# Attention values in three reduced-precision products per block, with split operands and smaller pools

## The chip, the cores and the metric

The kernel runs on one core of a Trainium2 chip. The core has a matrix engine (PE; its weight loads are shown apart as PEld), a vector engine (DVE), a scalar engine (ACT), a general engine (POOL), and an engine that here only issues DMAs (SP; its queue is SPq). Each takes its instructions in the order in which the program gives them. The metric is the device time of one execution in microseconds; a kernel's time is the median of several runs.

## The reference, cut to what matters

One step of a hybrid layer (a state-space branch, a differential-attention branch, a convolutional feed-forward part) runs over a prompt of 1024 positions and 64 sampled positions that have 512 cached ones. All arithmetic is in float32. The change lies in the attention:

```python
def _diff_attn_block(q, k, v, q_pos, k_pos, lam):
    s = jnp.einsum('bqhd,bkhd->bhqk', q, k) * (ATT_HEAD_DIM ** -0.5)
    s = jnp.where(visible[None, None], s, -jnp.inf)
    p = jax.nn.softmax(s, axis=-1).reshape(b, ATT_HEADS, 2, nq, -1)
    a = p[:, :, 0] - lam * p[:, :, 1]
    return jnp.einsum('bhqk,bkhe->bqhe', a.astype(v.dtype), v)
```

There are 8 heads; a head's values are 128 wide, and queries are taken in blocks of 128.

## The kernel before, in words

Names first. `F32` is float32; `R32` is a reduced form of it in the same four bytes. A product in full precision (both operands F32) is one instruction in the program and two MATMUL records in the trace. Where the kernel wants nearly full precision from R32 operands it splits each into a high part (a cast to R32, made on ACT) and a low part (the float32 value less the high part, made on DVE), and adds three products in one PSUM bank: high by high, high by low, low by high (`product`, L153 to L158). The input projections are all of this kind: one tile of 128 outputs by 384 or 320 positions is 8 times three MATMULs.

**Attention** (L659 to L821) goes head by head, and in a head over nine units, in the order of `ATT_ORDER`: unit i < 8 is the i-th block of 128 queries with 128(i+1) keys, unit 8 is the 64 sampled queries with 576 keys. `head_tiles` (L661) fetches a head's queries, keys and values; the values were `v_t` (nine blocks of 128 rows, two buffers) and `cv_t` (four blocks of cached values, one buffer). `attend` (L682) makes the scores with R32 operands (L707, L708, the high and the low part of the keys against the same stationary `q_t`), takes row maxima on DVE (L712, L716) and exponentials on ACT (L721, into `p_t`, four buffers), joins the two softmaxes on DVE (L725), and then, a step later, transposes the result by blocks of 128 keys on PE (L736, full precision, into the PSUM tile `pt`, four blocks to a tile), copies each `pt` to `a_t` (L741 on ACT and L743 or L745 on DVE, by turns) and multiplies it by the values (L755): one product of 128 moving columns a block, in full precision, with the block of `a_t` as the stationary operand. A head has 1+2+...+8 = 36 such blocks and 5 of unit 8, so 8 heads have 328. ACT then copies the sum out (L756) and squares it (L757). `head_out` (L760) norms a head's output, transposes it (L777), splits it (L780, L781) and stores it.

**What lies between.** Attention alone does not fill PE. `fill` draws from `stream()`, a row of projection tiles (convolution inputs, z, gates), 1.9 tiles a unit. Each is emptied from one of two PSUM banks by ACT or ACT and DVE; `conv_tiles` (L608) goes on from there with `pre` (two buffers) and `cc` (three), four DVE operations, one more ACT operation and a store on SP.

**Order.** The program is written in Python order, but a scheduler with its own table of costs puts the instructions of each engine into one fixed order when the kernel is built. So PE meets attention and projections interleaved in that order, and waits where an operand is late. Buffers of a pool are reused in turn, and a wait for a buffer stands in the queue of the engine that writes it next; for a DMA this is SP's queue, in which the loads of projection weights (`w_f`, L142) and the stores of `cc` (L635) stand too.

Of the kernel before, what the change touches and what calls it, by code (L numbers as in the profile page):

```python
# [9 lines left out]
F32 = mybir.dt.float32  # L10
R32 = mybir.dt.float32r
AF = mybir.ActivationFunctionType
ALU = mybir.AluOpType
# [4 lines left out]
P = 128  # L18
D = 1024
KT = D // P  # L20
TP, TS = 1024, 64
T = TP + TS
# [3 lines left out]
LAMBDA_INIT = 0.8 - 0.6 * math.exp(0.0)  # L26
# [21 lines left out]
QSQ = 1  # L48
QUICK = 400
IDLE = (9, 8)  # L50
AT = 4
AHEAD_IN = 100
AHEAD = 100
ZR = 3
# [16 lines left out]
O_FS, O_SUB, O_LAM = 408, 452, 580  # L71
# [4 lines left out]
def hybrid_layer(ctx: ExitStack, tc: tile.TileContext, xT, xN, prm, cst, rope, wvd, win, wbs, wba, wout, wup, wdn,  # L76
                 ckT, cv, st0, yT, kT, v, ssm, conv, ffn):
    nc = tc.nc
    V, S, G, PE = nc.vector, nc.scalar, nc.gpsimd, nc.tensor
    act = S.activation  # L80
    load = nc.sync.dma_start
# [16 lines left out]
    par = cp.tile([P, N_PRM], F32, name="par")  # L98
# [193 lines left out]
    with tc.tile_pool(name="nx", bufs=1) as nx:  # L292
# [116 lines left out]
        w = [raw_weights(wvd[0], 4, 272), raw_weights(wvd[1], 4, 272)]  # L409
# [7 lines left out]
        a, b = halves  # L417
# [166 lines left out]
    cv_pool = tc.alloc_tile_pool(name="cv", bufs=1, side="right")  # L584
# [23 lines left out]
    def conv_tiles(tiles):  # L608
        for f in tiles:
            tail = None  # L610

            def evac(ps, c, w):
                nonlocal tail
                n = min(w, TP - c)
                pre = cv_pool.tile([P, 387], F32, name="pre", tag="pre", bufs=2)
                cc = cv_pool.tile([P, 384], F32, name="cc", tag="cc", bufs=3)
                if tail is None:
                    G.memset(pre[:, 0:3], 0.0)  # L618
                else:
# [10 lines left out]
                act(cc[:, :m], pre[:, :m], AF.Identity, bias=col(O_CB + f), scale=cw(0))  # L630
# [4 lines left out]
                load(out=x_sc[P * f : P * (f + 1), c : c + n], in_=cc[:, :n])  # L635
# [23 lines left out]
    with (tc.tile_pool(name="ak", bufs=1) as ak, tc.tile_pool(name="at", bufs=1) as at,  # L659
          tc.tile_pool(name="psc", bufs=1, space=PSUM) as psc, tc.tile_pool(name="psa", bufs=1, space=PSUM) as pa):  # L660
        def head_tiles(h):  # L661
            def fetch(name, n, b, parts):
                t = ak.tile([P, n], R32, name=name, tag=name, bufs=b)
                for lo, src in parts:
                    load(out=t[lo : lo + src.shape[0]].bitcast(F32), in_=src)
                return t

            by_head = lambda d: [d.rearrange("(x h) t -> h x t", h=16)[2 * h + c] for c in range(2)]
            q, k, ck = by_head(q_st), by_head(k_st), by_head(c_st)
            q_t = [fetch("q_t", T, 3, [(0, q[0])]), fetch("q_t", T, 3, [(0, q[1][64:128]), (64, q[1][0:64])])]  # L670
            kh_t = [fetch("kh_t", T, 3, [(0, k[c][0:64]), (64, k[c][0:64])]) for c in range(2)]
            kl_t = [fetch("kl_t", T, 3, [(0, k[c][64:128]), (64, k[c][64:128])]) for c in range(2)]
            v_t = ak.tile([P, 9, P], F32, name="v_t", tag="v_t", bufs=2)
            load(out=v_t[:, :8], in_=v[0:TP, P * h : P * (h + 1)].rearrange("(a p) e -> p a e", p=P))
            load(out=v_t[:TS, 8], in_=v[TP:T, P * h : P * (h + 1)])
            ch_t = [fetch("ch_t", PAST, 2, [(0, ck[c][0:64]), (64, ck[c][0:64])]) for c in range(2)]
            cl_t = [fetch("cl_t", PAST, 2, [(0, ck[c][64:128]), (64, ck[c][64:128])]) for c in range(2)]
            cv_t = ak.tile([P, 4, P], F32, name="cv_t", tag="cv_t", bufs=1)
            load(out=cv_t, in_=cv[:, P * h : P * (h + 1)].rearrange("(a p) e -> p a e", p=P))
            return q_t, kh_t, kl_t, ch_t, cl_t, v_t, cv_t  # L680

        def attend(h, i, tiles, o_t, ssq, s0):  # L682
            q_t, kh_t, kl_t, ch_t, cl_t, v_t, cv_t = tiles
# [6 lines left out]
            for c in range(2):  # L690
# [7 lines left out]
                for a in range(0, nk, 512):  # L698
                    b = min(512, nk - a)
# [28 lines left out]
            nb = -(-nk // P)  # L728
            for b0 in range(0, nb, 4):
                pt = pa.tile([P, 512], F32, name="pt", tag="pt", bufs=2)  # L730
                a4 = at.tile([P, 512], F32, name="a_t", tag="a_t", bufs=AT)
                a_t.append(a4)
                full = 0
                for b in range(b0, min(nb, b0 + 4)):
                    kw = min(P, nk - b * P)
                    PE.transpose(pt[:kw, (b - b0) * P : (b - b0) * P + n], pr[1][:n, b * P : b * P + kw], ident[:n, :n])  # L736
                    full += kw == P
                m3 = lambda x, k: x.rearrange("p (a b) -> p a b", b=P)[:, :k, :n]
                if full:
                    if (i + b0 // 4) % 2:  # L740
                        S.copy(m3(a4, full), m3(pt, full))  # L741
                    else:
                        V.tensor_copy(m3(a4, full), m3(pt, full))  # L743
                else:
                    V.tensor_copy(a4[:TS, :n], pt[:TS, :n])  # L745
            po = pa.tile([P, 512], F32, name="po", tag="pt", bufs=2)
            for b in range(nb):
                kw = min(P, nk - b * P)
                if i < 8:
                    rhs = v_t[:, b]  # L750
                elif b < 4:
                    rhs = cv_t[:, b]
                else:
                    rhs = v_t[:TS, 8]
                PE.matmul(po[:n, :P], a_t[b // 4][:kw, b % 4 * P : b % 4 * P + n], rhs, start=b == 0, stop=b == nb - 1)  # L755
# [4 lines left out]
        def head_out(h, o_t, ssq, s0):  # L760
            ms, rs, t0, t1 = (at.tile([P, 9], F32, name=n, tag=n, bufs=2) for n in ("ms", "ors", "on0", "on1"))
            V.tensor_tensor(out=ms, in0=s0, in1=s0, op=ALU.mult)
            V.tensor_scalar(ms, ms, EPS * 128, None, ALU.mult)
            V.tensor_tensor(out=ms, in0=ms, in1=ssq, op=ALU.add)
            act(t0, ms, AF.Ln, scale=1.0 / 128)
            act(t0, t0, AF.Exp, scale=-0.5)
            V.tensor_scalar(ms, ms, -0.5 / 128, None, ALU.mult)
            V.tensor_tensor(out=ms, in0=ms, in1=t0, op=ALU.mult)
            V.tensor_tensor(out=t1, in0=ms, in1=t0, op=ALU.mult)
            V.scalar_tensor_tensor(rs, t1, 1.5, t0, ALU.add, ALU.mult)  # L770
            for b0 in range(0, 9, 4):
# [7 lines left out]
                hi, lo = (at.tile([P, 512], R32, name=n, tag="a_t", bufs=AT)[:, :w] for n in ("oh", "ol"))  # L779
                S.copy(hi, pt[:, :w])  # L780
                V.tensor_tensor(out=lo, in0=pt[:, :w], in1=hi, op=ALU.subtract)  # L781
# [5 lines left out]
        lt = at.tile([P, 512], F32, name="lt", tag="a_t", bufs=AT)[:, :64]  # L787
# [807 lines left out]
```

## Time and profile before

| | us |
|---|---|
| median of 3 runs | 2453.19 |
| lowest, highest run | 2453.03, 2457.49 |
| the profiled execution's own time | 2448.89 |
| its span, first to last instruction | 2447.1 |
| attention: first scores to last value product | 400.2 to 1080.0 |
| PE idle over the whole span (2447.1 less 2423.5 busy) | 23.6 |

The page divides the span by engine: share of time busy, and number of instructions. The views used below are: the busy time of every engine in given stretches; groups of instructions by line and shape (count, busy time, mean duration of one); who waited for whom; and the timeline (start, duration, engine, line, shape). A MATMUL's duration in the timeline covers its way through the array, so neighbours overlap; what one costs PE is the step from its start to the next one's start.

### The profile page before, as it was taken

The page shows a single profiled execution, that of the slowest core. Times are in us where ns is not written, and L with a number is a line of the kernel's source. Part 1 is how long each engine was busy: PE and PEld are TensorE (multiplying, and loading weights), DVE is VectorE, ACT ScalarE, POOL GpSimd, SP SyncE. Part 2 cuts the span into 40 slices and gives each one's busy share as a digit, 9 for nine tenths or more (in the row PEclk, how much of TensorE's full clock was granted, in tenths as well). Part 3 has the DMA queues.
Part 4 walks back from the last instruction along what each step waited for, and adds up shares of the span by engine and source line. Part 5 has one row for each costly group of instructions (what it writes and reads, how often), then busy time and mean ns, then how long its engine had stood idle before and what let it go on. Part 6 is the DMA issues. An engine that isn't in the chain of part 4 may idle for free. (4 is left out here: it accounts for less than half of the span.)

```text
span 2447.1 us, 44586 instructions
## 1 busy us (share of the span) xinstructions
PE 2423.5 (99%) x16956; PEld 2350.1 (96%) x16956; DVE 1602.0 (65%) x2755; ACT 1139.8 (47%) x2497; POOL 664.8 (27%) x696
## 2 busy tenths in 40 slices
PE   9999999999999999999999999999999999999998
PEld 8999999999999999999899989999999999999998
DVE  7426254865777667646767785656777777787766
ACT  6334243644565555437664653224543334353532
POOL 0000000100011001004333333103367666755434
PEclk9999999999999999999999999999999999999999
DMA  4218158554453453345679765656234343467874
GB/s 172 84 57 288 64 207 265 142 158 126 131 162 110 130 169 104 98 157 186 217 255 323 223 199 186 193 176 189 63 125 140 117 153 116 147 202 207 218 181 159
DMA packets 269319, 403.55 MB, mean 165 GB/s; under 512 B 33296, under 2 KB 202000, under 8 KB 268976
## 3 DMA queue, kind: packets, MB, share of 16 engines
q1 hardware_dynamic: 258432, 385.06, 49.6%
q0 software_dynamic: 4608, 8.91, 2.4%
q10 hardware_dynamic: 6064, 6.72, 0.8%
q8 instruction: 133, 2.18, 0.4%
q14 instruction: 82, 0.67, 0.1%
HBM read 267.04 MB, written 133.56 MB: 164 GB/s over the span
## 5 line engine op out<-in xcount | busy, mean ns | idle before, releaser
L156 PE MATMUL mm<-xn_hi,w_hi 128*128 128x384 f32 (+1 forms) x1416 | 469.9, 332 | 0.9 <-DVE zr L603 0.9
L158 PE MATMUL mm<-xn_hi,w_lo 128*128 128x384 f32 (+1 forms) x1416 | 468.6, 331 | 0.5 <-DVE w_lo L150 0.5
L157 PE MATMUL mm<-xn_lo,w_hi 128*128 128x384 f32 (+1 forms) x1416 | 467.7, 330 | 0.0
L156 PEld LDWEIGHTS mm<-xn_hi,w_hi 128*128 128x128 f32 x1416 | 266.7, 188 | 4.8 <-issue 1.6
L158 PEld LDWEIGHTS mm<-xn_hi,w_lo 128*128 128x128 f32 x1416 | 266.5, 188 | 3.4 <-issue 1.5
L157 PEld LDWEIGHTS mm<-xn_lo,w_hi 128*128 128x128 f32 x1416 | 266.7, 188 | 2.3 <-issue 1.1
L150 DVE TENSOR_TENSOR w_lo<-w_f,w_hi 128x1024 fp32r<-128x1024 f32 x116 | 147.1, 1270 | 117.9 <-ACT w_hi L149 117.5
L1254 PE MATMUL mx<-n,wh 128*128 128x272 f32 x1076 | 206.0, 289 | 0.7 <-ACT u L1398 0.4
L1254 PE MATMUL mx<-m,w_hi 128*128 128x272 f32 x1010 | 192.9, 289 | 4.2 <-DVE down L1412 4.2
L149 ACT CAST w_hi<-w_f 128x1024 fp32r<-128x1024 f32 x116 | 121.4, 1048 | 145.2 <-PE mm L157 87.5
L1254 PEld LDWEIGHTS mx<-n,wh 128*128 128x128 f32 x1076 | 169.2, 189 | 1.1 <-ACT u L1398 0.6
L1254 PEld LDWEIGHTS mx<-m,w_hi 128*128 128x128 f32 x1010 | 159.3, 189 | 4.6 <-issue 2.8
L1254 PE MATMUL mx<-n,wl 128*128 128x272 f32 x538 | 155.6, 289 | 0.0
L156 PE MATMUL mm<-b_hi,w_hi 128*128 128x384 f32 (+1 forms) x448 | 145.8, 327 | 0.6 <-DVE b_g L224 0.6
L1254 PE MATMUL mx<-m,w_lo 128*128 128x272 f32 x505 | 145.9, 289 | 0.0
L158 PE MATMUL mm<-b_hi,w_lo 128*128 128x384 f32 (+1 forms) x448 | 144.8, 324 | 0.6 <-DVE w_lo L150 0.6
L157 PE MATMUL mm<-b_lo,w_hi 128*128 128x384 f32 (+1 forms) x448 | 145.1, 325 | 0.0
L721 ACT ACTIVATE p_t<-sc,mx 128x1024 f32<-128x1024 f32 (+5 forms) x144 | 106.2, 739 | 76.4 <-DVE mx L712 37.5
L632 DVE SCALAR_TENSOR_TENSOR cc<-pre,par,cc 128x384 f32<-128x384 f32 (+1 forms) x216 | 126.6, 586 | 20.1 <-ACT cc L630 14.9
L620 POOL COPY pre<-pre 128x3 f32<-128x3 f32 x48 | 13.6, 282 | 454.5 <-ACT pre L621 343.6
L1039 ACT CAST w_hi<-ws 128x512 fp32r<-128x512 f32 (+1 forms) x62 | 37.6, 607 | 150.0 <-PE mx L1254 99.2
L618 POOL MEMSET pre<- 128x3 f32 x24 | 2.4, 101 | 383.9 <-PE mx L158 308.5
(418 smaller groups left out, 6735.7 us busy)
## 6 DMA issues: line engine op xcount, KB each, us to landing
w_f<-in_win_dram SPq DMA_DIRECT2D x76, 512.0 KB, 4.1
w_f<-in_wup_dram SPq DMA_DIRECT2D x44, 512.0 KB, 3.8
hr<-q_sc SPq DMA_DIRECT2D x70, 272.0 KB, 4.8
bc<-a_sc SPq DMA_DIRECT2D x32, 512.0 KB, 5.9
q_sc<-hb SPq DMA_DIRECT2D x44, 272.0 KB, 2.3
gb<-q_sc SPq DMA_DIRECT2D x44, 272.0 KB, 3.8
x_sc<-cc SPq DMA_DIRECT2D x48, 192.0 KB, 2.5
q_sc<-gb SPq DMA_DIRECT2D x33, 272.0 KB, 2.3
```

The costliest lines, as they stand in the source:

```text
L149: S.copy(hi, w)
L150: lowered = V.tensor_tensor(out=lo, in0=w, in1=hi, op=ALU.subtract)
L156: PE.matmul(ps, a_hi, b_hi, start=i == 0, stop=False)
L157: PE.matmul(ps, a_hi, b_lo, start=False, stop=False)
L158: PE.matmul(ps, a_lo, b_hi, start=False, stop=i == n - 1)
L618: G.memset(pre[:, 0:3], 0.0)
L620: G.tensor_copy(pre[:, 0:3], tail)
L632: V.scalar_tensor_tensor(cc[:, :m], pre[:, i : i + m], cw(i), cc[:, :m], ALU.mult, ALU.add)
L721: act(p_t[:n, :nk], sc[c][:n, :nk], AF.Exp, bias=mx[:n, c : c + 1], accum_out=dst)
L1039: S.copy(hi, src)
L1254: PE.matmul(ps, w[x][:, c], b[y][:, k], start=start and k == t == 0, stop=k == nk - 1 and t == 2, skip_group_check=not start)
```

## The change

The full-precision value product becomes three R32 products. For that, the transposed probabilities are split into `a_hi` (cast on ACT) and `a_lo` (difference on DVE), for every `pt`, where one copy on one of the two engines stood; and a head's values are split into `v_hi` and `v_lo`, once a head, 13 blocks of 128 rows each (prompt, cache, sample), in one buffer each. The float32 values that are split are loaded into two of the four `p_t` buffers. Where four `a_t` buffers stood, there are two `a_hi` and two `a_lo`. `cc` has two buffers in place of three, and the scaled norm weights `wsub` are made in place in `par`.

```diff
-AT = 4
+AT = 2
...
-                cc = cv_pool.tile([P, 384], F32, name="cc", tag="cc", bufs=3)
+                cc = cv_pool.tile([P, 384], F32, name="cc", tag="cc", bufs=2)
...
-            v_t = ak.tile([P, 9, P], F32, name="v_t", tag="v_t", bufs=2)
-            load(out=v_t[:, :8], in_=v[0:TP, P * h : P * (h + 1)].rearrange("(a p) e -> p a e", p=P))
-            load(out=v_t[:TS, 8], in_=v[TP:T, P * h : P * (h + 1)])
+            v_f = [at.tile([P, 8, P], F32, name="v_f", tag="p_t", bufs=4) for _ in range(2)]
+            load(out=v_f[0], in_=v[0:TP, P * h : P * (h + 1)].rearrange("(a p) e -> p a e", p=P))
+            load(out=v_f[1][:TS, 4], in_=v[TP:T, P * h : P * (h + 1)])
...
-            cv_t = ak.tile([P, 4, P], F32, name="cv_t", tag="cv_t", bufs=1)
-            load(out=cv_t, in_=cv[:, P * h : P * (h + 1)].rearrange("(a p) e -> p a e", p=P))
-            return q_t, kh_t, kl_t, ch_t, cl_t, v_t, cv_t
+            load(out=v_f[1][:, :4], in_=cv[:, P * h : P * (h + 1)].rearrange("(a p) e -> p a e", p=P))
+            v_t = [ak.tile([P, 13, P], R32, name=name, tag=name, bufs=1) for name in ("v_hi", "v_lo")]
+            for rows, to, src in ((P, slice(0, 8), v_f[0]), (P, slice(8, 12), v_f[1][:, :4]), (TS, slice(12, 13), v_f[1][:, 4:5])):
+                hi, lo = (t[:rows, to] for t in v_t)
+                S.copy(hi, src[:rows])
+                V.tensor_tensor(out=lo, in0=src[:rows], in1=hi, op=ALU.subtract)
+            return q_t, kh_t, kl_t, ch_t, cl_t, v_t
...
-                a4 = at.tile([P, 512], F32, name="a_t", tag="a_t", bufs=AT)
+                a4 = [at.tile([P, 512], R32, name=name, tag=name, bufs=AT) for name in ("a_hi", "a_lo")]
...
-                if full:
-                    if (i + b0 // 4) % 2:
-                        S.copy(m3(a4, full), m3(pt, full))
-                    else:
-                        V.tensor_copy(m3(a4, full), m3(pt, full))
-                else:
-                    V.tensor_copy(a4[:TS, :n], pt[:TS, :n])
+                hi, lo, src = (m3(t, full) if full else t[:TS, :n] for t in (*a4, pt))
+                S.copy(hi, src)
+                V.tensor_tensor(out=lo, in0=src, in1=hi, op=ALU.subtract)
...
-                PE.matmul(po[:n, :P], a_t[b // 4][:kw, b % 4 * P : b % 4 * P + n], rhs, start=b == 0, stop=b == nb - 1)
+                at_v = b if i < 8 else 8 + b
+                a_hi, a_lo = (t[:kw, b % 4 * P : b % 4 * P + n] for t in a_t[b // 4])
+                v_hi, v_lo = (t[:kw, at_v] for t in v_t)
+                PE.matmul(po[:n, :P], a_hi, v_hi, start=b == 0, stop=False)
+                PE.matmul(po[:n, :P], a_hi, v_lo, start=False, stop=False)
+                PE.matmul(po[:n, :P], a_lo, v_hi, start=False, stop=b == nb - 1)
...
-        wsub = at.tile([P, P], F32, name="wsub")
-        V.tensor_scalar_mul(wsub, par[:, O_SUB : O_SUB + P], 1.0 - LAMBDA_INIT)
+        wsub = par[:, O_SUB : O_SUB + P]
+        V.tensor_scalar_mul(wsub, wsub, 1.0 - LAMBDA_INIT)
```

The scheduler lays the changed program out anew between the first scores and the last value product; before and behind this stretch PE's instructions stand as they did, but for some just behind it. Two places follow.

The first is PE at the first value products of the first head (unit 7). In the names of the rows, `mm` is a projection tile, `sc` scores, `po` the sum of the value products. Before:

```order
L156 MATMUL mm<-xn_hi_89,w_hi 128x384
L157 MATMUL mm<-xn_lo_90,w_hi 128x384
L755 MATMUL po<-v_t,a_t 128x128 [waits DMAHW6_49,Activation_49]
L755 MATMUL po<-v_t,a_t 128x128 x3
L707 MATMUL sc<-kh_t,q_t 128x256 [waits Activation_49]
L755 MATMUL po<-v_t,a_t 128x128 [waits DVE_49]
L755 MATMUL po<-v_t,a_t 128x128 x3
```

And the same place in the changed kernel:

```order
L158 MATMUL mm<-xn_hi_89,w_lo 128x384
L156 MATMUL mm<-xn_hi_91,w_hi 128x320 [waits Activation_49]
L157 MATMUL mm<-xn_lo_92,w_hi 128x320
L752 MATMUL po<-v_hi,a_hi 128x128 [waits DVE_49]
L753 MATMUL po<-v_lo,a_hi 128x128
L754 MATMUL po<-v_hi,a_lo 128x128
```

The triple of the last three rows then stands once for each block. Between the unit's last transpose and its first value product stood 21 projection MATMULs; now 26 stand there, and four of the scores. Counted over all heads, the 984 value MATMULs of the changed kernel stand in 157 unbroken runs, and 152 of these follow a projection or score MATMUL of at least 256 columns.

The second place is ACT at the change from the first head to the second, in the changed kernel (`o_t` and `po` are the first head's last unit, `p_t` the second head's second):

```order
L725 ACTIVATE p_t,s_4421<-sc,mx 128x128 [waits DVE_49]
L755 COPY o_t<-po 128x128 [waits PE_49]
L756 ACTIVATE po,ssq<-po 128x128
L682 CAST v_hi<-v_f 128x1024 [waits DMAHW4_49]
L682 CAST v_hi<-v_f 128x512 [waits DMAHW7_49]
L682 CAST v_hi<-v_f 64x128 [waits DMAHW6_49]
```

These casts are new in ACT's order; each waits for a DMA. In SP's queue these DMAs stand as follows; the loads of `v_t`, which had two buffers, waited for no more than the products of an earlier head:

```order
L674 DMA v_f<-out_dram 128x8x128 [waits DMAHW4_49,DVE_49,Activation_49]
L635 DMA x_sc<-cc 128x384 [waits DMAHW5_49,DVE_49]
L675 DMA v_f<-out_dram 64x128 [waits DMAHW6_49,PE_49]
L678 DMA v_f<-in_cv_dram 128x4x128 [waits DMAHW7_49]
L635 DMA x_sc<-cc 128x384 [waits DMAHW0_49,DVE_49]
```

The loads of values now wait for a `p_t` buffer (DVE, ACT, PE) and have stores of `cc` between them and behind them.

More of the change, by code (lines that the diff above doesn't have):

```diff
@@ L672, in head_tiles @@
             kl_t = [fetch("kl_t", T, 3, [(0, k[c][64:128]), (64, k[c][64:128])]) for c in range(2)]
-            v_t = ak.tile([P, 9, P], F32, name="v_t", tag="v_t", bufs=2)
-            load(out=v_t[:, :8], in_=v[0:TP, P * h : P * (h + 1)].rearrange("(a p) e -> p a e", p=P))
-            load(out=v_t[:TS, 8], in_=v[TP:T, P * h : P * (h + 1)])
+            v_f = [at.tile([P, 8, P], F32, name="v_f", tag="p_t", bufs=4) for _ in range(2)]
+            load(out=v_f[0], in_=v[0:TP, P * h : P * (h + 1)].rearrange("(a p) e -> p a e", p=P))
+            load(out=v_f[1][:TS, 4], in_=v[TP:T, P * h : P * (h + 1)])
             ch_t = [fetch("ch_t", PAST, 2, [(0, ck[c][0:64]), (64, ck[c][0:64])]) for c in range(2)]
             cl_t = [fetch("cl_t", PAST, 2, [(0, ck[c][64:128]), (64, ck[c][64:128])]) for c in range(2)]
-            cv_t = ak.tile([P, 4, P], F32, name="cv_t", tag="cv_t", bufs=1)
-            load(out=cv_t, in_=cv[:, P * h : P * (h + 1)].rearrange("(a p) e -> p a e", p=P))
-            return q_t, kh_t, kl_t, ch_t, cl_t, v_t, cv_t
+            load(out=v_f[1][:, :4], in_=cv[:, P * h : P * (h + 1)].rearrange("(a p) e -> p a e", p=P))
[5 more added lines that the diff above has]
+            return q_t, kh_t, kl_t, ch_t, cl_t, v_t
         def attend(h, i, tiles, o_t, ssq, s0):
-            q_t, kh_t, kl_t, ch_t, cl_t, v_t, cv_t = tiles
+            q_t, kh_t, kl_t, ch_t, cl_t, v_t = tiles
             n = min(P, T - i * P)
@@ L778, in head_out @@
                 w = min(T, top * P) - b0 * P
-                hi, lo = (at.tile([P, 512], R32, name=n, tag="a_t", bufs=AT)[:, :w] for n in ("oh", "ol"))
+                hi, lo = (at.tile([P, 512], R32, name=n, tag=n, bufs=AT)[:, :w] for n in ("a_hi", "a_lo"))
                 S.copy(hi, pt[:, :w])
@@ L786, in hybrid_layer @@
         lam = at.tile([P, 4], F32, name="lam")
-        lt = at.tile([P, 512], F32, name="lt", tag="a_t", bufs=AT)[:, :64]
-        wsub = at.tile([P, P], F32, name="wsub")
-        V.tensor_scalar_mul(wsub, par[:, O_SUB : O_SUB + P], 1.0 - LAMBDA_INIT)
+        lt = at.tile([P, 512], F32, name="lt", tag="a_hi", bufs=AT)[:, :64]
+        wsub = par[:, O_SUB : O_SUB + P]
+        V.tensor_scalar_mul(wsub, wsub, 1.0 - LAMBDA_INIT)
         for i in range(2):
```

6 lines of the change are left out of this document (removed).

## The prediction

> **What bounds the kernel now.** I read the page's first part, then the busy time by stretches, then PE's waits.
>
> ```profile
> span 2447.1 us, 44586 instructions
> PE 2423.5 (99%) x16956; PEld 2350.1 (96%) x16956; DVE 1602.0 (65%) x2755; ACT 1139.8 (47%) x2497; POOL 664.8 (27%) x696
> 425.00:1085.00 660.00, 658.72 (x4248) 634.71 (x4247) 446.10 (x967) 360.43 (x910) 47.73 (x137) 1.00 0.44 130
> 400.00:1090.00 690.00, 90.68 (x656) 83.86 (x656) 1.00 0.46 136
> PE sc L708 <- DMA kl_t<-k_st: 3.3, 3, 2.0
> PE sc L707 <- DMA kh_t<-k_st: 1.3, 1, 1.3
> PE sc L707 <- issue: 0.5, 1, 0.5
> ```
>
> PE is busy 99% of the span. The third row is the attention stretch (its length, then busy us of PE, PEld, DVE, ACT, POOL, then granted clock, DMA share, GB/s): PE has 1.3 us of idle in 660, with DVE at 68% and ACT at 55%. The fourth row is L755, the value product, alone: 656 records, 90.68 us; with 328 blocks that is two records a block, as full precision has. The last three rows are all that PE waited between 400 and 1090 us (total, times, longest), at the stage's start. No copy to `a_t` was ever late. So whatever PE has to do more here is added to the time, and whatever it is spared is taken off; ACT and DVE work counts only where it makes PE stand.
>
> **What a value product costs PE.** A busy PE is not PE at its peak, so I take steps from start to start.
>
> ```profile
> 440.40 0.34 PE L158 MATMUL mm<-xn_hi,w_lo 128*128 128x384 f32 x1
> 440.57 0.83 PE L755 MATMUL po<-v_t,a_t 128*128 128x128 f32 x6
> 441.24 0.38 PE L736 MATMUL pt<-con,p_t 128*128 128x128 f32 x2
> 468.64 0.19 PEld L708 LDWEIGHTS sc<-kl_t,q_t 128*128 128x128 f32 x1
> 468.75 0.19 PEld L707 LDWEIGHTS sc<-kh_t,q_t 128*128 128x128 f32 x1
> 468.70 0.28 PE L708 MATMUL sc<-kl_t,q_t 128*128 128x128 f32 x1
> 468.81 0.28 PE L707 MATMUL sc<-kh_t,q_t 128*128 128x128 f32 x1
> 468.92 0.28 PE L708 MATMUL sc<-kl_t,q_t 128*128 128x128 f32 x1
> 469.04 0.39 PE L158 MATMUL mm<-xn_hi,w_lo 128*128 128x384 f32 x1
> 446.82 0.40 PE L708 MATMUL sc<-kl_t,q_t 128*128 128x512 f32 x1
> 447.05 0.22 PE L707 MATMUL sc<-kh_t,q_t 128*128 128x128 f32 x1
> 447.11 0.27 PE L708 MATMUL sc<-kl_t,q_t 128*128 128x128 f32 x1
> 447.22 0.40 PE L158 MATMUL mm<-xn_hi,w_lo 128*128 128x384 f32 x1
> ```
>
> *Before.* Three blocks (x6) take 441.24 − 440.57 = 0.67 us, so a block costs 0.223 us, two steps of 0.112.
>
> *After.* The new product, R32 with 128 stationary and 128 moving columns, has a twin in the trace: the scores of units 0 and 4, whose last key block is 128 wide. Four in a row at 468.56: the steps from 468.70 are 0.11, 0.11, 0.12, that is 0.34 for three, 0.113 each. That is not what 128 moving columns take: the 384-column MATMUL steps by 0.17 (440.40 to 440.57), the 512-column one by 0.23 (446.82 to 447.05), so 128 columns alone take 0.23 / 4 = 0.057. At 447.05 a 128-column MATMUL does cost 0.06, and the next one 0.11. The weight loads explain both: at 468.64 and 468.75 they start 0.11 apart, and behind a 512-column MATMUL the load is already done. So a short R32 product costs a weight load, 0.112 us, save the first of a run behind a wide MATMUL, which costs 0.06. The scores at 468.70 and 468.64 show one thing more: L707 and L708 of one softmax share the stationary `q_t`, and each loads it. The first two new products share `a_hi` in the same way; I count three loads.
>
> The Trainium skill says in "TensorE: Matmul & The Clock Gate", LDWEIGHTS, that a load's time goes by the stationary columns, their number over 1.2 GHz, 107 ns for 128; the trace agrees with 112 ns. By that figure the full-block term below would be 288 × (3 × 0.107 − 0.223) = +28 us, an estimate.
>
> **The sum on PE.**
> - 8 heads × 36 = 288 full blocks: 3 × 0.112 = 0.336 for 0.223, +0.113 each, **+32.5 us**.
> - 152 of the 157 runs of value products start behind a wide MATMUL and find their first weights loaded: 152 × (0.112 − 0.06) = **−7.9 us**. Before, nothing was hidden so: the full-precision product's own streaming fills its step.
> - 8 × 5 = 40 blocks of the sampled unit have 64 stationary columns, whose R32 products step by 0.02 and 0.06 in the rows below. Three cost 0.18 by the larger step, for 0.22: **−1.6 us**. Bounds: −6 by the smaller step, +4.5 if they cost as the full ones.
>
> ```profile
> 445.37 0.19 PE L707 MATMUL sc<-kh_t,q_t 128*64 128x64 f32 x1
> 445.39 0.22 PE L708 MATMUL sc<-kl_t,q_t 128*64 128x64 f32 x1
> 445.45 0.42 PE L157 MATMUL mm<-xn_lo,w_hi 128*128 128x384 f32 x1
> ```
>
> Together +23 us on PE. If no run finds its weights loaded it is +31, if each step is 0.107 and the small blocks go by the smaller step, +14.
>
> **Other parts, and what covers them.**
>
> ```profile
> L743 DVE COPY a_t<-pt x56: 273/555/694, 421.6 to 1066.1; 128x512 f32<-128x512 f32 x24, 128x256 f32<-128x256 f32 x16, 128x128 f32<-128x128 f32 x8, 128x384 f32<-128x384 f32 x8
> L780 ACT CAST oh<-pt x24: 191/587/602, 492.4 to 1105.6; 128x512 fp32r<-128x512 f32 x16, 128x64 fp32r<-128x64 f32 x8
> L781 DVE TENSOR_TENSOR ol<-pt,oh x24: 201/676/692, 493.8 to 1106.2; 128x512 fp32r<-128x512 f32 x16, 128x64 fp32r<-128x64 f32 x8
> L149 ACT CAST w_hi<-w_f x39: 1032/1048/1062, 435.1 to 1084.3; 128x1024 fp32r<-128x1024 f32 x39
> L150 DVE TENSOR_TENSOR w_lo<-w_f,w_hi x38: 1199/1224/1228, 437.5 to 1070.6; 128x1024 fp32r<-128x1024 f32 x38
> ```
>
> Splitting `pt`: 112 tiles (before, 48 copies on ACT, 64 on DVE) now take a cast on ACT (0.59 at 512 columns) and a difference on DVE (0.68), by these rows 64 casts and 48 differences more, under 64 × 0.59 = 38 us on ACT and 48 × 0.68 = 33 us on DVE. Splitting the values: 8 heads × (1.05 + 0.59 + 0.19) = 15 us on ACT, 8 × (1.22 + 0.68 + 0.20) = 17 us on DVE. DVE goes from 446 to under 496 us and ACT from 360 to under 413, in a stretch of 660 + 23: 73% and 60%. Neither becomes the bound, and PE's cover is the projections drawn between. The chain is longer: transposes, cast 0.59, difference 0.68 give 1.3 us, and 3.7 us if two of DVE's 1.22 differences stand ahead. The difference waits for ACT's cast, and behind it on DVE stand row maxima and the work on `cc`, for which ACT waits. The first head's first unit puts 26 MATMULs of some 0.17 us, over 4 us, in between. I take 0; cover gone, each of 112 tiles could cost up to 1.
>
> The loads of the values wait for `p_t` buffers; the casts wait for the loads, and on ACT the emptying of projection banks is queued behind them. The value products of the next head come only after a unit or more of other work. At the stage's start there is no such lead: I take **+3 us** for it, between 0 and the 7 us from the first `cl_t` load to the landing of `cv_t`:
>
> ```profile
> 406.19 4.09 SPq L665 DMA_DIRECT2D cl_t<-c_st  x4
> 410.31 0.59 SPq L679 DMA_DIRECT2D cv_t<-in_cv_dram  x1
> DMA to landing us min/median/max: 3.3/3.3/3.3
> ```
>
> `cc` with two buffers: a tile waits until the store of the last but one has landed. ACT filled the first three at 402.65, 413.88 and 417.74, and the first store left at 418.49: the third would start 3 us late. ACT's wait for `cc` was 1.9 us already with three; a delay under one tile's 24 × 0.17 = 4.1 us on PE is covered by the second bank. I take 0, with up to 5 in the range. `wsub` and the other moved lines issue the same work once: 0.
>
> ```profile
> 402.65 0.71 ACT L630 ACTIVATE cc<-pre,par 128x384 f32<-128x384 f32 x1
> 413.88 0.71 ACT L630 ACTIVATE cc<-pre,par 128x384 f32<-128x384 f32 x1
> 417.74 0.66 ACT L630 ACTIVATE cc<-pre,par 128x323 f32<-128x323 f32 x1
> 418.49 0.33 SPq L635 DMA_DIRECT2D x_sc<-cc  x1
> ACT cc L630 <- DMA x_sc<-cc: 1.9, 1, 1.9
> ```
>
> Sum: +23 + 3 = **+26 us**. The profiled execution took 2448.89 us, so 2475; the median of the runs lies 4.3 us above it at 2453.19, and there it makes **2479 us**, +1.06%.
>
> **Rivals.** A measurement of this kernel can tell about 0.2%, 4.9 us, from no change.
>
> *Moving columns decide (faster).* If PE pulled the weights far enough ahead, a product would cost its 0.057 for 128 columns, three 0.171 against 0.223 (about 4 × 0.057): 328 × −0.052 = −17, so 2436. For it: the 0.06 step behind a wide MATMUL. Against: three steps of 0.11 in a row, in the very shape. The Trainium skill, "FP8 and Floating Point Precision", TensorE Precision Notes, counts true float32 as four passes through the array, which would make three passes the cheaper; the 0.223 agrees with four, and the 0.113 steps say that the new ones would not be bound by passes. Chance 0.07.
>
> *The shared weights stay (faster).* If `a_hi` were loaded once for its two products, the second would cost 0.057: a block 0.112 + 0.057 + 0.112 = 0.281, +0.058 × 288 = +17, less 7.9 and 1.6, +7, or if the spared load lets the next one start early, 0.224 and −9, so between 2444 and 2460. Against it are the equal counts of MATMULs and loads on the page, 16956 of both. Chance 0.06, half of it faster, half unchanged or slower.
>
> *Waits take over (much slower).* At each change of heads the landing of the values decides. `v_t` landed after 4.0 us in the median and 10.3 at most:
>
> ```profile
> DMA to landing us min/median/max: 3.4/4.0/10.3
> 406.28 0.53 PE L157 MATMUL mm<-xn_lo,w_hi 128*128 128x384 f32 x1
> 406.60 0.53 PE L158 MATMUL mm<-xn_hi,w_lo 128*128 128x384 f32 x1
> 400.00:410.00 10.00, 7.32 (x29) 6.55 (x30) 3.10 (x5) 2.85 (x5) 0.19 (x1) 0.83 0.89 213
> ```
>
> If each comes 6.3 us late where ACT stands before its cast, PE's other bank covers 4.1, PE stands 2.2, and then runs slow: after the idle of 400 to 410 us the granted clock was 0.83 there and 384 columns stepped by 0.32 for nine MATMULs, 9 × 0.15 = 1.3 us more. 8 × 3.5 = 28, so 2507. It decides once a landing is later than a tile's 4.1 us. For it: the new waits in front of the loads. Against: not one wait for a value load before, and the loads stand a unit ahead. Chance 0.13.
>
> **How the numbers follow.** The chance of the forecast, weight loads decide and waits stay small, is 0.74; its own range is 2463 (+14 and no stall, a little less for the median) to 2499 (+31, +7, +5 and a few late differences). Rivals 0.07, 0.06 and 0.13. Likeliest 2479. For 8 in 10, 2462 to 2502: it leaves out the faster rivals, 0.10, and the worse part of the waits, some 0.08. Slower by over 0.2%: 0.74 + 0.13 + 0.01 = 0.88; within 0.2%: 0.02; faster: 0.07 + 0.03 = 0.10.
>
> **What would show it.** Right: L752, L753 and L754 with some 984 MATMULs and as many loads, steps of 0.11 inside a run and 0.06 at its start, busy 110 to 120 us in place of 90.68; PE still without idle in the stretch, which grows by some 25 us, and the stages behind it equal in length. Wrong: steps of 0.06 inside runs; fewer loads than MATMULs; PE waits named after `a_lo`, `v_lo` or a value load of more than 10 us in total.

## The result, and the profile after

| | before | changed |
|---|---|---|
| median, us (6 runs each, side by side) | 2452.99 | 2490.56 |
| lowest, highest | 2448.00, 2457.49 | 2487.36, 2496.62 |
| profiled execution, us | 2448.89 | 2487.36 |
| last value product ends, us | 1080.3 | 1112.1 |
| from there to the end of the span, us | 1366.8 | 1373.5 |

The ratio of the medians is 1.0153, with a 95% interval from 1.0142 to 1.0164: the change costs 37.6 us, where 26 were forecast. Of the 38.5 us by which the two profiled executions differ, 31.8 lie before the end of the last value product and 6.7 behind it.

First the page's own lines for the changed kernel, its span and the busy time of each engine:

```profile
span 2485.6 us, 45386 instructions
PE 2455.5 (99%) x17284; PEld 2381.0 (96%) x17284; DVE 1641.0 (66%) x2827; ACT 1171.6 (47%) x2585; POOL 664.9 (27%) x696
```

PE has 328 MATMULs more (17284 for 16956) and as many loads as MATMULs: 984 value products of one record each stand where there were 656 records of full precision. PE was 99% busy before and is so still.

Next, the attention stretch from 400 us to the end of the last value product (to within 0.1 us), as busy time by engine (PE, PEld, DVE, ACT, POOL, then clock, DMA share, GB/s). The kernel before:

```profile
400.00:1080.20 680.20, 676.24 (x4335) 651.16 (x4336) 459.29 (x990) 366.29 (x923) 49.74 (x143) 1.00 0.46 134
```

The changed kernel, and below it the same stretch with the value products alone:

```profile
400.00:1112.00 712.00, 706.31 (x4666) 682.00 (x4667) 496.37 (x1063) 399.23 (x1012) 53.24 (x143) 1.00 0.44 128
400.00:1112.00 712.00, 122.98 (x984) 1.00 0.44 128
```

The stretch grew by 31.8 us. PE's busy time in it grew by 30.1, and its idle time (length less busy) from 4.0 to 5.7 us. So nearly all of it is time in which PE works, not waiting. DVE is at 496 of 712 us (70%) and ACT at 399 (56%): neither has become the bound.

What PE waited for between 400 and 1120 us in the changed kernel (total, times, longest) is this, the whole list:

```profile
PE sc L712 <- DMA kl_t<-k_st: 2.3, 2, 2.1
PE mm L156 <- DVE zr L603: 1.7, 2, 1.4
PE sc L711 <- DMA kh_t<-k_st: 1.3, 1, 1.3
PE sc L711 <- ACT p_t L725: 1.0, 1, 1.0
PE sc L711 <- issue: 0.5, 1, 0.5
```

No row names `a_hi`, `a_lo`, `v_hi`, `v_lo` or a value load, so no split operand was late for PE. The kernel before had no wait for `p_t` or `zr` here, and 3.3 us for `kl_t`: of the 1.7 us more of idle, the new waits make 2.7, and `kl_t` takes 1.0 off. The wait for `p_t` has its cause on ACT, whose rows stand first here:

```profile
424.04 0.66 ACT L630 ACTIVATE cc<-pre,par 128x323 f32<-128x323 f32 x1 [5.12 <-DMA x_sc<-cc]
424.61 0.99 ACT L725 ACTIVATE p_t<-sc,mx 128x896 f32<-128x896 f32 x1
425.74 0.39 PE L711 MATMUL sc<-kh_t,q_t 128*128 128x256 f32 x1 [1.00 <-ACT p_t L725]
```

ACT stood 5.12 us for a free `cc` buffer (the bracket gives the idle time before a row and what ended it), the exponential of the scores came behind, and PE stood 1.0 us for it.

Then one run of value products, in PE's timeline of the changed kernel (start, duration, engine, line, shape). Four blocks of three stand between a projection and a score MATMUL:

```profile
441.26 0.34 PE L158 MATMUL mm<-xn_hi,w_lo 128*128 128x384 f32 x1
441.44 0.22 PE L752 MATMUL po<-v_hi,a_hi 128*128 128x128 f32 x1
441.50 0.28 PE L753 MATMUL po<-v_lo,a_hi 128*128 128x128 f32 x1
441.61 0.27 PE L754 MATMUL po<-v_hi,a_lo 128*128 128x128 f32 x1
441.72 0.27 PE L752 MATMUL po<-v_hi,a_hi 128*128 128x128 f32 x1
...
442.61 0.27 PE L754 MATMUL po<-v_hi,a_lo 128*128 128x128 f32 x1
442.72 0.39 PE L711 MATMUL sc<-ch_t,q_t 128*64 128x512 f32 x1
```

The first step is 0.06 and the eleven others are 0.11: (442.72 − 441.50) / 11 = 0.111. That is the pattern the prediction drew from four score MATMULs. The sampled unit's products have the same 128 moving columns but 64 stationary ones:

```profile
473.17 0.23 PE L754 MATMUL po<-v_hi,a_lo 128*64 128x128 f32 x1
473.23 0.22 PE L752 MATMUL po<-v_hi,a_hi 128*64 128x128 f32 x1
473.30 0.22 PE L753 MATMUL po<-v_lo,a_hi 128*64 128x128 f32 x1
```

They step by 0.06, as 94 of the 96 of this shape do. Half the stationary columns, at the same moving columns, take about half the time: the weights, not the moving columns, set the price of the full blocks.

But look at what follows a run when it is a projection. Two value products, and the three 384-column MATMULs behind them, in the changed kernel:

```profile
443.27 0.31 PE L752 MATMUL po<-v_hi,a_hi 128*128 128x128 f32 x1
443.42 0.28 PE L753 MATMUL po<-v_lo,a_hi 128*128 128x128 f32 x1
443.53 0.39 PE L156 MATMUL mm<-xn_hi,w_hi 128*128 128x384 f32 x1
443.75 0.34 PE L157 MATMUL mm<-xn_lo,w_hi 128*128 128x384 f32 x1
443.93 0.35 PE L158 MATMUL mm<-xn_hi,w_lo 128*128 128x384 f32 x1
```

The one at 443.53 steps by 0.22, the next by 0.18 (0.17 is the usual step of this shape). It was already to be seen before: the last row of the prediction's four scores and projection, at 447.22, is followed in the kernel before by

```profile
447.46 0.34 PE L156 MATMUL mm<-xn_hi,w_hi 128*128 128x384 f32 x1
447.63 0.34 PE L157 MATMUL mm<-xn_lo,w_hi 128*128 128x384 f32 x1
```

so that it took 0.24 and not 0.17. A run between two wide products thus saves 0.05 us at its start and pays as much behind its end. The second is not the first come back: the run at 443.27 stands behind a narrow score product, its first step is 0.15 and saves nothing, and the wide product behind it is longer all the same. The four scores that the prediction read show it too: their first step, from 468.56, is 0.14, and the projection behind them steps by 0.22 (469.04 to 469.26).

I added up the steps of all value products from start to start, and what a product of 320 to 512 columns that stands right behind a run takes beyond the usual of its shape:

| us | before | changed | difference |
|---|---|---|---|
| full blocks (128 stationary columns) | 60.3 | 90.3 | +30.0 |
| blocks of the sampled unit (64) | 11.0 | 9.0 | −2.0 |
| pushed into the wide product behind the run | 4.7 (54 runs) | 5.5 (96 runs) | +0.7 |
| together | 76.0 | 104.8 | **+28.8** |

If each of the 864 products cost 0.111, the full blocks would take 95.9; they took 90.3, and 5.5 is paid behind them. The net gain from short first steps is 0.1 us.

Last, what ACT waited for in the changed kernel between 400 and 1120 us, the two rows on what the change moved:

```profile
ACT cc L630 <- DMA x_sc<-cc: 28.7, 15, 5.1
ACT v_hi L682 <- DMA v_f<-out_dram: 5.5, 1, 5.5
```

ACT stood 28.7 us for a free `cc` buffer (1.9 before) and 5.5 us for the first head's values. One of these waits is seen to reach PE, the one at 424.04; what the rest costs is a question for the experiments.

### The profile page after: what moved, and what is told of

Its sections match the earlier page's. It is cut to its first block, busy times and chain, and to the rows that moved or that the text cites. A ratio compares the mean times of both kernels' runs of the same rounds, so it can differ in the third digit from the quotient of the medians.

```text
span 2485.6 us, 45386 instructions
## 1 busy us (share of the span) xinstructions
PE 2455.5 (99%) x17284; PEld 2381.0 (96%) x17284; DVE 1641.0 (66%) x2827; ACT 1171.6 (47%) x2585; POOL 664.9 (27%) x696
## 4 chain that ended last, share of the span: by engine, by line
PE 49%; DVE 3%; DMA 3%; ACT 2%; issue 1%; SPq 1%; POOL 0%; DVEq 0%; ACTq 0%; POOLq 0%
PE mx L1253 17%; PE mm L1253 7%; PE mm L156 4%; PE mm L158 4%; PE mm L157 4%; PE mx L156 2%; PE mx L158 2%; PE mx L157 2%; DMA hr<-q_sc 1%; PE mx L1313 1%; PE yi L872 1%; PE ye L878 1%; PE stp L884 1%; PE mm L1313 1%; DMA b_f<-y_sc 1%
## 5 line engine op out<-in xcount | busy, mean ns | idle before, releaser
L632 DVE SCALAR_TENSOR_TENSOR cc<-pre,par,cc 128x384 f32<-128x384 f32 (+1 forms) x216 | 126.7, 587 | 40.0 <-ACT cc L630 37.6
L620 POOL COPY pre<-pre 128x3 f32<-128x3 f32 x48 | 19.0, 396 | 469.1 <-ACT pre L621 190.6
L725 ACT ACTIVATE p_t<-sc,mx 128x1024 f32<-128x1024 f32 (+5 forms) x144 | 106.7, 742 | 49.0 <-DVE p_t L729 25.4
L1038 ACT CAST w_hi<-ws 128x512 fp32r<-128x512 f32 (+1 forms) x62 | 37.6, 606 | 147.7 <-PE mx L1253 100.6
```

The lines of the kernel that those rows point to most:

```text
L725: act(p_t[:n, :nk], sc[c][:n, :nk], AF.Exp, bias=mx[:n, c : c + 1], accum_out=dst)
L1038: S.copy(hi, src)
```

## The experiments

Theory: a short R32 product costs its weight load, 0.111 us, so three cost 0.336 where one full-precision block cost 0.223. Rivals: the moving columns set the price; the two products with `a_hi` share a load, or would if they stood otherwise; the smaller `cc` pool or the splitting, not the products, took the time. Ratios below are to the kernel before, run on the same chip.

**One product in full precision, all the rest of the change kept.**

```diff
-  v_t = [ak.tile([P, 13, P], R32, ...) for name in ("v_hi", "v_lo")]
+  v_t = [ak.tile([P, 13, P], F32 if name == "v_hi" else R32, ...) for name in ("v_hi", "v_lo")]
...
-  PE.matmul(po[:n, :P], a_hi, v_hi, start=b == 0, stop=False)
-  PE.matmul(po[:n, :P], a_hi, v_lo, start=False, stop=False)
-  PE.matmul(po[:n, :P], a_lo, v_hi, start=False, stop=b == nb - 1)
+  PE.matmul(po[:n, :P], a_hi, v_hi, start=b == 0, stop=b == nb - 1)
```

(`a_hi` likewise in F32; the casts, the differences and all pools stay.)

> The changed kernel with one full-precision product per block instead of three; the casts and differences of probabilities and values, the two buffers each, the two cc buffers and the loads through p_t all stay (the differences are all zero and are not multiplied). If the three products are the whole price: the time of before, 2453, within 5 us. If the smaller pools, the new waits or the work on ACT and DVE carry a part: 2458 or more, up to 2468.

Measured: 2463.04 us (2459.07 to 2466.55), ratio 1.0040 [1.0026, 1.0054]. So 27.5 of the 37.6 us go with the products, and about 10 stay with something else in the change. Its attention stretch:

```profile
400.00:1089.40 689.40, 680.11 (x4335) 650.13 (x4335) 493.09 (x1062) 399.79 (x1011) 55.76 (x143) 1.00 0.45 132
```

PE's idle is 9.3 us here, more than in the changed kernel (5.7), though DVE and ACT do the same work. I read this as less cover: with less work on PE, a late operand shows sooner.

**The third product left out.** `a_lo` by `v_hi` is not computed; `a_lo` is still made.

```diff
-  PE.matmul(po[:n, :P], a_hi, v_lo, start=False, stop=False)
-  PE.matmul(po[:n, :P], a_lo, v_hi, start=False, stop=b == nb - 1)
+  PE.matmul(po[:n, :P], a_hi, v_lo, start=False, stop=b == nb - 1)
```

> The third product (low part of the probabilities by high part of the values) is left out of the result; its operand is still made. If each product costs a weight load of 0.112 us: 288 x 0.112 + 40 x 0.06 = 35 us less than 2490.6, about 2456. If it costs its 128 moving columns, 0.057: 328 x 0.057 = 19 us less, about 2472.

Measured: 2458.48 us (2455.99 to 2462.77), ratio 1.0027 [1.0015, 1.0038], 32 below the changed kernel. A weight load for each of 328 products predicted 35, moving columns 19. The steps agree: the value products take 66.9 us here for 99.3 (the first two rows of the table above), which is 32.4 less.

**The order of the products changed**, so that the two that share `a_hi` no longer stand together.

```diff
-  PE.matmul(po[:n, :P], a_hi, v_lo, start=False, stop=False)
-  PE.matmul(po[:n, :P], a_lo, v_hi, start=False, stop=b == nb - 1)
+  PE.matmul(po[:n, :P], a_lo, v_hi, start=False, stop=False)
+  PE.matmul(po[:n, :P], a_hi, v_lo, start=False, stop=b == nb - 1)
```

> The three products in the order high-high, low-high, high-low, so that no two neighbours have the same stationary block. If every product loads its own weights anyway: no change, 2490.6 within 4 us. If neighbours with the same a_hi shared a load, or part of one: up to 288 x 0.055 = 16 us more, 2506.

Measured: 2492.16 us (2488.89 to 2492.53), ratio 1.0154 [1.0139, 1.0169]; the changed kernel has 1.0153. In the timeline:

```profile
442.65 0.27 PE L752 MATMUL po<-v_hi,a_hi 128*128 128x128 f32 x1
442.76 0.27 PE L753 MATMUL po<-v_hi,a_lo 128*128 128x128 f32 x1
442.88 0.28 PE L754 MATMUL po<-v_lo,a_hi 128*128 128x128 f32 x1
442.99 0.27 PE L752 MATMUL po<-v_hi,a_hi 128*128 128x128 f32 x1
```

The steps are 0.11 or 0.12 in either order: two neighbours with the same weights save nothing, so there was nothing to lose. (This order says nothing of the moving columns, which it leaves as they were.)

**Two loads a block instead of three.** `v_hi` and `v_lo` lie side by side; `a_hi` meets both at once in 256 columns, and DVE adds the halves at the end of a unit.

```diff
-  PE.matmul(po[:n, :P], a_hi, v_hi, start=b == 0, stop=False)
-  PE.matmul(po[:n, :P], a_hi, v_lo, start=False, stop=False)
-  PE.matmul(po[:n, :P], a_lo, v_hi, start=False, stop=b == nb - 1)
+  PE.matmul(po[:n, : 2 * P], a_hi, v_both, start=b == 0, stop=False)
+  PE.matmul(po[:n, :P], a_lo, v_both[:, :P], start=False, stop=b == nb - 1)
```

> High and low values lie side by side, and a_hi meets both in one MATMUL of 256 moving columns; a_lo by high follows with 128. The two halves are added on DVE once a unit. Moving columns are the same, weight loads two instead of three. If loads decide: a block 0.118 + 0.112 = 0.23 for 0.336, 288 x 0.106 = 30 us less, about 2460. If moving columns decide: no change, 2490.

Measured: 2490.79 us (2488.52 to 2493.44), ratio 1.0152 [1.0137, 1.0167]. The forecast of 2460 missed by 30, and the time alone is what the rival of the moving columns gives. The timeline decides against that rival: the block did become as cheap as the theory says.

```profile
1105.86 0.33 PE L752 MATMUL po<-v_both,a_hi 128*128 128x256 f32 x1
1106.03 0.22 PE L753 MATMUL po<-v_both,a_lo 128*128 128x128 f32 x1
1106.09 0.33 PE L752 MATMUL po<-v_both,a_hi 128*128 128x256 f32 x1
```

A block steps by 0.23 (1105.86 to 1106.09), about the 0.223 of the full-precision one. In all, the value products took 75.7 us (PE's idle between them left out) where the changed kernel has 99.3. Over the whole span PE is busy 16.0 us less than in the changed kernel (2439.5 for 2455.5) and stands 20.0 us more (50.1 for 30.1). Busy time by engine in the last stretches of the attention of this kernel:

```profile
1050.00:1100.00 50.00, 37.42 (x206) 32.77 (x206) 28.88 (x70) 24.57 (x63) 0.00 (x0) 0.81 0.14 47
1100.00:1140.00 40.00, 35.70 (x212) 33.10 (x211) 18.28 (x42) 16.56 (x50) 0.00 (x0) 0.94 0.18 53
```

and in the changed kernel:

```profile
1050.00:1100.00 50.00, 50.00 (x337) 48.30 (x336) 24.96 (x53) 20.61 (x59) 0.00 (x0) 1.00 0.22 66
```

PE stands 12.6 us of 50, and its granted clock drops to 0.81, where the changed kernel has no idle. The scheduler had laid the projections further forward: by the fixed order of the two programs, 279 projection MATMULs stand behind the last head's first value product in the changed kernel, and 113 in this one. With these used up, the last head's units wait for their own softmax (PE's idle there is put down to ACT's `p_t`, L725, as in the 1.21 us just before 1104.38). So the run shows the price of a block, and that PE's cover is a stock that can be spent too early; it doesn't show what the cheaper block is worth when projections are left for the last head.

**Two `cc` buffers in the kernel before, nothing else.**

```diff
-                cc = cv_pool.tile([P, 384], F32, name="cc", tag="cc", bufs=3)
+                cc = cv_pool.tile([P, 384], F32, name="cc", tag="cc", bufs=2)
```

> The kernel before with two cc buffers in place of three and nothing else changed. If the missing buffer carries the 10 us that one full-precision product with all other parts of the change cost: 2458 to 2463. If it is hidden, as the prediction had it: 2453 within 3.

Measured: 2462.37 us (2458.69 to 2463.23), ratio 1.0036 [1.0023, 1.0049]: +9.5. This one line, with the new order that the scheduler gives the program for it, is worth what `one_full` had left over. Its attention stretch, two rows of PE's waits and one of ACT's:

```profile
400.00:1090.80 690.80, 678.29 (x4335) 651.29 (x4336) 459.76 (x990) 366.03 (x923) 46.95 (x143) 1.00 0.45 132
PE mm L156 <- ACT pre L621: 3.9, 1, 3.9
PE sc L707 <- ACT p_t L721: 3.1, 2, 2.4
ACT cc L630 <- DMA x_sc<-cc: 30.3, 13, 7.2
```

ACT waits 30.3 us for `cc`, once 7.2 at a stretch, and behind it stand `pre`, which empties a projection bank for PE, and the exponentials. PE's idle is 12.5 us, for 4.0.

**One product alone, no low parts**: neither `a_lo` nor `v_lo` is made, and only `a_hi` by `v_hi` is computed. Once with two `cc` buffers, once with three, for which there is room without the low parts.

```diff
-  PE.matmul(po[:n, :P], a_hi, v_hi, start=b == 0, stop=False)
-  PE.matmul(po[:n, :P], a_hi, v_lo, start=False, stop=False)
-  PE.matmul(po[:n, :P], a_lo, v_hi, start=False, stop=b == nb - 1)
+  PE.matmul(po[:n, :P], a_hi, v_hi, start=b == 0, stop=b == nb - 1)
```

> The changed kernel with the high parts alone: one R32 product a block, no differences made of probabilities or values (the low parts are left out of the result). Pools of p_t, cc and the high parts as in the change. Against the run with two products (2458.5) one product less. If a product costs a weight load: 35 us less, 2424. If it costs its moving columns: 19 less, 2440.

> As the run with the high parts alone, with three cc buffers, which fit when the low parts are gone. If the third cc buffer is worth what was lost: 4 to 9 us less than the high parts alone, about 2417. If not: the same within 3.

Measured: 2433.45 us (2429.59 to 2437.50), ratio 0.9921 [0.9907, 0.9935], and with three buffers 2420.94 us (2417.83 to 2423.16), ratio 0.9873 [0.9857, 0.9889]. Their attention stretches, with two buffers:

```profile
400.00:1058.00 658.00, 644.01 (x4007) 613.48 (x4007) 429.73 (x926) 395.63 (x1011) 55.32 (x143) 0.99 0.48 139
```

and with three, with ACT's wait for `cc`:

```profile
400.00:1042.90 642.90, 635.54 (x4007) 610.60 (x4007) 430.62 (x926) 397.32 (x1011) 54.01 (x143) 1.00 0.49 142
ACT cc L630 <- DMA x_sc<-cc: 0.6, 1, 0.6
```

From two products to one the time fell by 25, between the 35 of loads and the 19 of columns: by itself this step tells nothing, because stalls grew at the same time (PE's idle is 14.0 us, 10.2 with two products). The steps do tell: the value products take 32.3 us here for 66.9, 34.6 less, which is the price of loads. With the third buffer the time falls by 12.5, more than the 4 to 9 expected. The attention is 15.1 us shorter: PE's idle falls by 6.6, to 7.4, and its busy time by 8.5 for the same 4007 MATMULs, while the granted clock rises from 0.99 to 1.00. It looks as if standing was paid for twice, as idle and as slower work behind it. With less work on PE the buffer is worth more: 12.5 us here, 9.5 in the kernel before. Among the kernels tried this is the fastest, 32 us below the one before; it is no substitute for it, since the low parts are missing from its values.

**The changed kernel profiled a second time**, with no edit at all.

> The changed kernel as it stands, profiled once more, for the 6.7 us that it lost behind the last value product. If this belongs to the program: the last stage is again 4 us longer than before, with PE waiting for the sums of the down projection. If it is chance: within 1.5 us of before.

Measured: 2489.42 us in its one run. The attention took 716.8 us (712.0 the first time), the rest 1370.8 (1373.5). In the attention 1.7 of the 4.8 us are idle and 3.1 are longer busy time for the same 4666 MATMULs: the granted clock was 0.83 from 400 to 410 us, 0.93 from 420 to 430 and 0.90 from 430 to 440, where the first execution had 1.00. Before 428.45 us PE had stood 2.1 us for `p_t`. Behind the attention, 2.7 of the 6.7 us differ between two executions of one program, and 3.9 came again, which speaks for the program by the expectation; but PE's waits for the sums of the down projection grew only from 4.2 to 5.6 us.

**The stores of `cc` issued by POOL instead of SP**, in the changed kernel, and as a control in the kernel before with two `cc` buffers.

```diff
-                load(out=x_sc[...], in_=cc[:, :n])
+                G.dma_start(out=x_sc[...], in_=cc[:, :n])
...
-                    load(out=x_sc[...], in_=cc[:, n + 3 : m])
+                    G.dma_start(out=x_sc[...], in_=cc[:, n + 3 : m])
```

> The changed kernel with the stores of cc (L635, L637) issued by POOL instead of SP; nothing is left out. ACT's wait for a cc buffer was 28.7 us in the changed kernel. If the missing third buffer costs the changed kernel what it costs the kernel before by itself (9.4 us) and if the stores come late because they stand behind loads on SP, ACT's wait falls below 10 us and the time falls by 7 to 10, to about 2482. If PE's cover (its idle in the attention is 5.7 to 7.4 us, against 4.0 before) leaves only 2 to 3 us of it, the wait falls and the time falls by no more than 4, to 2486 to 2491. If the wait doesn't fall, the stores are slow for another reason and the time says nothing of cc.

> The kernel before with two cc buffers and with the stores of cc issued by POOL; nothing is left out. Control for the run beside it. cc_two alone was +9.4 on the kernel before, with ACT waiting 30.3 us for cc. If these waits are stores that stand behind loads on SP, the wait falls below 10 us and the time comes back to 2453 to 2456. If the wait stays at 30 us, 2462.

Measured: the control takes 2454.12 us (2448.46 to 2457.09), ratio 0.9998 [0.9988, 1.0009]. Everything that the missing buffer cost has come back, without the buffer. The wait fell less than expected (below 10 us), and its longest from 7.2 to 2.4 us; so it is not shown that the stores were late because they stood behind loads on SP:

```profile
400.00:1080.80 680.80, 675.89 (x4335) 649.30 (x4334) 459.41 (x990) 365.69 (x923) 97.58 (x239) 1.00 0.46 134
ACT cc L630 <- DMA x_sc<-cc: 17.3, 14, 2.4
```

The changed kernel with these stores takes 2486.74 us (2484.86 to 2491.79), ratio 1.0136 [1.0117, 1.0156], that is +33.0. The rows of its profile:

```profile
400.00:1111.40 711.40, 706.89 (x4666) 683.21 (x4667) 498.27 (x1063) 400.64 (x1012) 101.69 (x239) 1.00 0.44 128
ACT cc L630 <- DMA x_sc<-cc: 28.5, 17, 4.9
```

ACT's wait did not fall here, so by what I had written down the run says nothing of `cc`. It does show two things. PE's idle is 4.5 us, 0.5 over the kernel before, and the attention is still 31.2 us longer: 30.7 of it is longer busy time of PE, so it is the work of the products and not waiting that makes it longer. And ACT's 28.5 us of waiting for `cc` cost PE next to nothing in this program. The medians put 4 us between this kernel and the changed one, but their intervals overlap.

## Why the prediction was right, and where its size was off

**What bounds the kernel: right.** PE stayed at 99%, and the attention grew by PE's work: +30.1 us busy, +1.7 idle.

**The price of a product: right.** 0.113 was read from four score MATMULs; 0.111 is what the new ones step by. Full blocks, with what all runs push behind them, cost +30.7 us, against the forecast +32.5. The Trainium skill's figure for a load of 128 columns, 107 ns ("TensorE: Matmul & The Clock Gate", LDWEIGHTS), is 4% below the 0.111, and the estimate that the prediction drew from it was +28 us. `two` and `wide` confirm the price from both sides: a product less saves 32 us, a load less brings the block to 0.23.

**Three loads, none shared: right.** `apart` and the equal counts show it, and the rival of shared weights falls. That of the moving columns falls by `two` (32 us, where it gave 19), and by the 0.06 for 64 stationary columns beside the 0.111 for 128.

**The hidden first loads, −7.9 us: this is the step that failed.** The prediction took "152 × (0.112 − 0.06)" as a gain. The 0.06 steps are there, but the wide product behind a run is longer by as much, 0.05 to 0.06 us behind nearly all of the 96 runs. This price stands at the end of a run, whatever its start was, and the prediction had no term for it. "Before, nothing was hidden so" holds for the start of a full-precision run, whose first step is 0.11. At its end the last record steps by only 0.03 in 51 of 90 runs of full blocks, and the wide product behind is longer by 0.08: the full blocks are 3.9 us shorter than 0.223 each, and all runs push 4.7. The net is nil after the change and a small loss before it, so the sum on PE is near the bound the prediction named for this case, +31; 28.8 were measured. The first row that shows it, 447.46, was the next one after the rows that I quoted, and 469.26 would have followed the four scores: I took the step at a run's start and did not look at the one behind its end.

**The small blocks, −1.6 us: right**, −2.0, though by two errors of one size: a block took 0.275 before and takes 0.225 now, where 0.22 and 0.18 were taken. The 0.06 held for 94 of the 120 products.

**Splits at nothing: right.** DVE and ACT took 37 and 33 us more in the attention, under the forecast ceilings of 50 and 53, and PE never waited for a split operand in the changed kernel. The margin was not wide: in `apart`, where the same work stands in another order, it waited 3.1 us in all for `a_hi`.

**The start of the stage, +3 us: of the right size at most.** ACT waited 5.5 us for the first values, but no wait of PE is put down to them. From 400 to 430 us PE stood 3.7 us, for 2.7 before, and 5.0 in the second execution: 1.0 and 2.4 us more, most of it the wait for `p_t` behind `cc`. The first value product came 2.7 us later than before, but 138 MATMULs stand from the first score up to it, where 119 stood.

**`cc` with two buffers, "I take 0": the number nearly held, the reason did not.** The cover was to be the second PSUM bank, for delays under 4.1 us. But single waits reach 5.1 us in the changed kernel and 7.2 in `cc_two`, where the line alone costs 9.5 us. And the operand that was late for PE at 425.74 was not a projection bank but the exponential of the scores, for which the second bank is no cover. In the changed kernel most of the 9.5 is gone: PE's idle is 5.7 us, and 7.4 when profiled again, for 4.0 before. Its new waits thus cost a net 1.7 to 3.4 us of idle; 1.0 and 2.1 us of them stand behind a wait for `cc`. The changed kernel was not run with three buffers, so what `cc` alone costs it stays open. That a slower PE covers the waits of a smaller pool agrees with `one_full` (idle 9.3) and the two kernels without low parts, but it was not tried by itself.

**The stages behind, "equal in length": off.** They took 6.7 us more in one execution, 3.9 in the second and 4.8 in `store_pool`, and 1.0 in `one_full`. It is mostly PE standing there: 16.7, 15.4 and 16.6 us, for 11.4 before and 11.8 in `one_full`, over several short waits. This is the other part of the missing 12 us. Its cause stays open.

The account of the profiled execution is then: products +28.8, attention's idle +1.7, what is left in its busy time +1.3, stages behind +6.7, together 38.5; forecast were 23, 3, 0 and 0. What is left is not traced further. It may be 1.3 us larger, since the kernel before ran slow at 400 to 410 us (granted clock 0.83, the nine MATMULs of the prediction) and this execution did not (1.00). The rival "waits take over" did not come about: no head's values made PE wait.

## What to carry to other kernels

Where PE is the bound, count a short product by its weight load: splitting one full-precision product of 128 columns into three reduced ones adds a half to its cost here (0.336 for 0.223), and in `wide` a wider moving operand brought the block back to 0.23. When a step looks shorter at the start of a run, read the step behind the run's end too before booking the gain. Price a smaller buffer pool by the longest wait and by what is queued behind the waiting engine, and try the queue of its stores before paying for another buffer.

## What was not expected of the hardware

- A wide MATMUL behind a run of short R32 products is longer by 0.05 to 0.06 us (443.53: 0.22 for a usual 0.17), also where the run's first step was long. The 512-column score products with 128 stationary columns are lengthened too (six, by 0.05); the one with 64, at 442.72, is not (0.23, its usual step).
- At the same 128 moving columns, an R32 product steps by 0.111 us with 128 stationary columns and by 0.06 with 64.
- A 256-column R32 product followed by a 128-column one steps by 0.17 and 0.06, together 0.23: the columns of three products for little more than two loads (0.222).
- The same 96 stores of `cc` cost the kernel before 9.5 us with two buffers when SP issued them, and nothing when POOL did, though from issue to landing they took no less: 2.4 us in the median for 2.0.
- In `wide`, the granted clock was 0.81 over 50 us in which PE idled 12.6 us; in the same stretch of the changed kernel, without idle, it was 1.00. In the second execution of the changed kernel it was 0.93 from 420 to 430 us and 0.90 from 430 to 440, with 2.1 us of idle up to 428.45.
